# Two trunk layers in one kernel: grouped RWKV state products, values in the activation ring, reordered first loads, last gain on ScalarE

## The chip, the cores and the metric

The kernel runs on one core of one Trainium2 chip. The metric is the device time of one execution in microseconds; lower is better. The engines are TensorE (PE in the profile, PEld its weight loads), VectorE (DVE), ScalarE (ACT), GpSimd (POOL) and SyncE (SP, which only issues transfers here).

## What is computed

A sequence of 512 tokens of width 1024 goes through two layers, in float32. Each layer adds to the residual stream h a token mixer, a cross attention to a memory of 256 tokens, and a gated feed-forward block (1024 to 2 x 2752 and back, with a causal convolution of three taps). The first mixer is a gated linear attention (GLA, 4 heads) beside RWKV-7 (8 heads of 64); the second is an RG-LRU beside an mLSTM. The parts that the change touches are, cut to what matters:

```python
mem_n = rms_norm(mem, mem_norm_g)
# rwkv7_chunked, chunks of 64 tokens, per head:
rhs = concat([a_dec, A_ak @ v])
sol = triangular_solve(I - A_ab, rhs)
def step(S, inp):
    z = z_state @ S + z_local
    y = r_dec @ S + A_rb @ z + y_local
    S = S * decay + z^T b_end + v^T k_end
# the end of the trunk:
return rms_norm(h, final_norm_g)
```

## The kernel before

Activations lie transposed: a tile holds 128 features (partitions) by 512 tokens. A dense product is made of blocks: `block` (L261) loads one weight block of 128 x 1024 with `wload` (L240), which splits it into a rounded high part (`wh`, on ACT) and a remainder (`wl`, on DVE), and `dense` (L252) adds 24 products of 128 x 512 into a PSUM bank, three for each of eight feature tiles. A block's raw weights lie in a ring of 3 buffers (`wr`, "raw"), the parts in a ring of 2 (`wh`, `wl`), the PSUM banks of dense products in a ring of 3 (`mm`); 5 more banks (`ax`) serve everything else. Activations of the mixers lie in a ring of 16 buffers (`qr`, named "xs").

The program is written as straight Python, and a list scheduler puts the instructions of each engine into an order when the kernel is built: an instruction whose inputs and buffers are there by the scheduler's own reckoning goes next, earlier program text first. `issue_after(ins)` adds an edge: what is traced under it stands behind `ins` on the same engine. On the chip each engine and each transfer queue runs its order without looking ahead.

The stages that the change touches, in the order of time:

- Start (`Trunk.__init__` L144 to L183, `trunk` L1239 to L1269). SP loads the vector table, the first tile of x, the first weight block `wk` of 512 KB, then x1 to x7. POOL issues the load of `cmat` (identity, `bo64`, `rmask`). Ten products of `ones_d` by itself (L170) keep PE at work before the first weights are there. DVE scales `bo64` into `bo64m` (L178). Then `gla` (L593) runs, for each of eight feature tiles of x, two small "stacked" products and three of the first block; next come the sums of squares of x (`squares`, L1259), the reciprocal norm `rstd`, and `al` (tile "alr", L627), which frees a PSUM bank.
- The RWKV preparation (L800 to L869), four times, once for a pair of heads: blocks for r, k and v, gates, decays by a scan on DVE, score products. v is written into a zero-padded tile `vp` (L798, one buffer) at an offset of 64 columns, and nine transposes of overlapping windows (L832 to L839) bring the values of both heads into the tiles `SV`, by five copies on ACT. `during(p)` (L1281) puts other work in between: `memory_norm` (L484) loads four tiles of the memory, squares them on ACT and adds the squares on DVE, with its scratch in the `qr` ring.
- A triangular solve on DVE (L880 to L909) beside the key and value products of the memory.
- The state recurrence (L917 to L949): eight chunks, one after the other. A chunk has four groups of eight small products, over `p` (four pairs of heads) and `e` (the two heads of a pair): w (L922), the first part of y (L927), z (L931), uu (L938) and the last part of y (L947, which adds to the same bank as L927). z goes back into `SV[0]` by a DVE copy and into `SV[1]` by an ACT copy (L932, L933). A float32 product is two instructions in the trace, so a group is 16. Beside the recurrence PE works on dense products of the memory (`memory_k`, `memory_v`, called from `after`, L1293), which the scheduler puts between the groups.
- The end (`ffn` with `out`, L386 to L396, and `finish`, L1336). The last output block is made in two halves of 256 tokens. For each, `finish` forms the norm and multiplies eight tiles by gain and norm (L1347, eight DVE instructions of 128 x 256), and every second one issues a store of two tiles, in turn from SP and ACT.

Of the kernel before, what the change touches and what calls it, by code (L numbers as in the profile page):

```python
# [8 lines left out]
F32 = mybir.dt.float32  # L9
F32R = mybir.dt.float32r  # L10
U8 = mybir.dt.uint8
AF = mybir.ActivationFunctionType
ALU = mybir.AluOpType
# [4 lines left out]
P = 128  # L18
T = 512
# [123 lines left out]
class Trunk:  # L143
    def __init__(self, ctx, tc, I):  # L144
        self.tc, self.nc, self.I = tc, tc.nc, I
        nc = tc.nc
        self.con = self.pool(ctx, "con", 1)
        self.wr = self.pool(ctx, "wr", 3)
        self.wh = self.pool(ctx, "wh", 2)
        self.pr = (self.pool(ctx, "pa", 8), self.pool(ctx, "pb", 8))  # L150
        self.qr = self.pool(ctx, "qr", 16)
        self.mm = self.pool(ctx, "mm", 3, space=PSUM)
        self.ax = self.pool(ctx, "ax", 5, space=PSUM)
        self.dram = self.pool(ctx, "dr", 1, space=DRAM)
        con = self.con
        self.vec = con.tile([P, NVEC], F32, name="vec")
        nc.sync.dma_start(out=self.vec, in_=I["vec"])
        self.cm = con.tile([P, 384], F32, name="cmat")
        nc.gpsimd.dma_start(out=self.cm, in_=I["cmat"][:, 0:384])
        self.ident = self.cm[:, 0:128]  # L160
        self.bo64 = self.cm[:, 128:256]
        self.rmask = self.cm[:, 256:384]
        self.ones = {}
        for n, v in (("d", 1.0 / D), ("h", 1.0 / P)):
            t = con.tile([P, P], F32, name="ones_" + n)
            nc.gpsimd.memset(t, v)
            self.ones[n] = t

        warm = self.mm.tile([P, T], F32, name="mm")
        for i in range(10):  # L170
            self.mmul(warm[:, 0:P], self.ones["d"], self.ones["d"])
        self.cols = {}
        for n, v in (("eps", EPS), ("one", 1.0), ("gn", 64 * 1e-5), ("l2", 1e-12), ("tiny", 2e-38)):
            t = con.tile([P, 1], F32, name="col_" + n)
            nc.gpsimd.memset(t, v)
            self.cols[n] = t
        self.bo64m = con.tile([P, P], F32, name="bo64m")
        nc.vector.tensor_scalar(out=self.bo64m, in0=self.bo64, scalar1=1.0 / 64.0, scalar2=None, op0=ALU.mult)  # L178
        self.u = []
        for i in range(2):  # L180
            t = con.tile([P, T + 4], F32, name=f"upad{i}")
            nc.gpsimd.memset(t[:, 0:4], 0.0)
            self.u.append(t)  # L183
# [53 lines left out]
                self.nc.scalar.preload_act_table_set(name)  # L237


    def wload(self, src, kb, m):  # L240
        nc = self.nc
        raw = self.wr.tile([P, 1024], F32, name="raw")
        hi = self.wh.tile([P, 1024], F32R, name="wh")
        lo = self.wh.tile([P, 1024], F32R, name="wl")
        n = kb * m
        self.last_load = nc.sync.dma_start(out=raw[:, :n], in_=src.rearrange("p k m -> p (k m)"))
        self.act(hi[:, :n], raw[:, :n], AF.Copy)
        self.tt(lo[:, :n], raw[:, :n], hi[:, :n].bitcast(F32), ALU.subtract)
        sh = lambda t: t[:, :n].rearrange("p (k m) -> p k m", m=m)
        return sh(hi), sh(lo)  # L250

    def dense(self, ps, W, X, first=True, last=True):  # L252
# [43 lines left out]
class Norm:  # L296
# [5 lines left out]
    def feed(self, k, h):  # L302
        if self.ring is not None:
            self.operand(k, h)
        self.square(h)
# [178 lines left out]
def memory_norm(K, sm):  # L484

    nc = K.nc
    src = K.I["memT"].rearrange("(k p) m -> p k m", p=P)
    pair = lambda t: t.rearrange("p (k m) -> p k m", m=256)
    acc, M = sm.tile([P, T], F32, name="nacc"), []
    for i in range(4):  # L490
        f = K.qr.tile([P, T], F32, name="xs")
        nc.sync.dma_start(out=pair(f), in_=src[:, 2 * i:2 * i + 2])
        M.append(f)
        sq = K.qr.tile([P, T], F32, name="xs") if i else acc
        K.act(sq, f, AF.Square)
        if i:
            K.add(acc, acc, sq)
    yield M
    ps = K.mm.tile([P, T], F32, name="mm")
    for i in range(2):  # L500
        K.mmul(ps[:, 0:256], K.ones["d"], acc[:, i * 256:(i + 1) * 256], i == 0, i == 1)
    r = K.qr.tile([P, T], F32, name="xs")[:, 0:256]
    K.act(r, ps[:, 0:256], AF.Ln, bias=K.cols["eps"])
    K.act(r, r, AF.Exp, scale=-0.5)
    for k in range(KD):
        f = pair(M[k // 2])[:, k % 2]
        K.stt(f, f, K.v("mem_norm_g", k), r, ALU.mult, ALU.mult)
    yield M
# [84 lines left out]
def gla(K, nm, wga, wk, squares, after, Y):  # L593
    nc, X = K.nc, nm.X
    with ExitStack() as es:
# [4 lines left out]
        nc.gpsimd.dma_start(out=gf, in_=K.I["cmat"][:, 1024:1152].rearrange("p (o m) -> p o m", o=1))  # L600
        with K.tc.issue_after(after.ins):
            nc.vector.tensor_copy(out=gm, in_=gf)
        wa = gp.tile([48, 256], F32, name="walpha")
        nc.gpsimd.memset(wa, 0.0)
        for r in (0, 32):
# [147 lines left out]
def shifted(K, out, ps, i, om):  # L753

    K.act(out, ps, AF.Copy, scale=om[:, i:i + 1])
    K.stt(out[:, 1:], ps[:, 0:T - 1], K.v("rwkv_mu", i), out[:, 1:], ALU.mult, ALU.add)
    return out
# [9 lines left out]
def rwkv(K, X, Y, during, after):  # L767
# [3 lines left out]
    with ExitStack() as core:  # L771
# [12 lines left out]
        with ExitStack() as es:  # L784
# [10 lines left out]
            gl = shifted(K, new(), K.block("w_rw", 13, X), 13, om)  # L795
            sigmoid(K, glr, gl, scale=-1.0)
            reset = reset_mask(K, wt, 65)
            vp = wt.tile([P, 640], F32, name="vp")  # L798
            nc.gpsimd.memset(vp, 0.0)
            for p in range(4):  # L800
                r = shifted(K, new(), K.block("w_rw", p, X), p, om)
                k = shifted(K, new(), K.block("w_rw", 4 + p, X), 4 + p, om)
                v = shifted(K, vp[:, 64:576], K.block("w_rw", 8 + p, X), 8 + p, om)
                ps = K.ax.tile([P, T], F32, name="ax")
                psa = K.ax.tile([P, T], F32, name="ax")
                K.mmul(ps, w2a2[0:64, p * P:(p + 1) * P], wa[0:64])
# [22 lines left out]
                for e in range(2):  # L829
                    K.stt(stk[e][R[e], p, :, 0:64], c8(kn)[R[e]], -1.0, e1[R[e], :, 0:64], ALU.mult, ALU.mult)  # L830
                    K.mul(stk[e][R[e], p, :, 64:128], c8(r)[R[e]], e1[R[e], :, 1:])
                for w0, w1 in ((0, 4), (4, 8), (8, 9)):  # L832
                    ps = K.ax.tile([P, 4, P], F32, name="ax")
                    for w in range(w0, w1):
                        nc.tensor.transpose(ps[:, w - w0], vp[:, w * 64:w * 64 + P], K.ident)
                    if w0 < 8:
                        K.act(SV[0][64:128, w0:w1, p], ps[64:128, :, 0:64], AF.Copy)
                    w = max(w0, 1)
                    K.act(SV[1][0:64, w - 1:w1 - 1, p], ps[0:64, w - w0:w1 - w0, 64:128], AF.Copy)  # L839
                K.mul(kn, kn, a)  # L840
                K.act(a, a, AF.Identity, scale=K.v("rwkv_k_a", p), bias=om[:, 14 + p:15 + p])
                K.mul(k, k, a)
# [67 lines left out]
        with ExitStack() as es:  # L910
# [3 lines left out]
            for e in range(2):  # L914
                nc.vector.memset(SV[e][R[e], 0], 0.0)
            yt = [st.tile([P, T], F32, name=f"y{p}", bufs=1) for p in range(4)]
            for c in range(8):  # L917
                w = K.ax.tile([P, 4, 64], F32, name="ax")
                yp = K.ax.tile([P, 4, 64], F32, name="ax")
                for p in range(4):  # L920
                    for e in range(2):
                        K.mmul(w[R[e], p], stk[e][:, p, c, 0:64], SV[e][:, c, p])  # L922
                ws = st.tile([P, 4, 64], F32, name="ws")
                nc.vector.tensor_copy(out=ws, in_=w)
                for p in range(4):
# [7 lines left out]
                K.act(SV[1][R[1], c], z[R[1]], AF.Copy)  # L933
                if c < 7:
                    uu = K.ax.tile([P, 4, 64], F32, name="ax")
                    for p in range(4):
                        for e in range(2):
                            K.mmul(uu[R[e], p], BKT[:, p, c, R[e]], SV[e][:, c, p])  # L938
                    t = st.tile([P, 4, 64], F32, name="t")
                    K.add(t, S, uu)  # L940
                    sb = sdt[:, c].rearrange("p (a o) -> p a o", o=1)
                    for e in range(2):
                        K.mul(SV[e][R[e], c + 1], t[R[e]], sb[R[e]].to_broadcast([64, 4, 64]))
                    K.mul(S, t, sb.to_broadcast([P, 4, 64]), nc.gpsimd)
                for p in range(4):
                    for e in range(2):
                        K.mmul(yp[R[e], p], SV[e][R[e], c, p], BB[R[e], p, c, 64:128], False, p == 3)  # L947
                for p in range(4):
                    K.act(yt[p][:, c * 64:c * 64 + 64], yp[:, p], AF.Copy)  # L949
            g2 = K.qr.tile([P, T], F32, name="xs")  # L950
# [288 lines left out]
def trunk(tc, I, out):  # L1239
    nc = tc.nc  # L1240
    with ExitStack() as ctx:
        K = Trunk(ctx, tc, I)
        sm = K.pool(ctx, "nsm", 1)
        with ExitStack() as es:
# [4 lines left out]
            load = lambda k: nc.sync.dma_start(out=x[k], in_=I["xT"][k * P:(k + 1) * P])  # L1249
            load(0)  # L1250
            alpha = stacked_weights(K, I["w_ga"][:, 0], 16, 32, nt.tile([P, KD * 48], F32R, name="walr", bufs=1), nc.scalar)
            wk = K.wload(I["w_gla"][:, 2], KD, P)
            for k in range(1, KD):
                load(k)
            K.exp_ln()
            for k in range(KD):
                last = nm.operand(k, x[k])
# [50 lines left out]
        for l in range(2):  # L1308
# [23 lines left out]
            else:  # L1332
# [3 lines left out]
                def finish(s, ps):  # L1336
# [6 lines left out]
                    K.mmul(ms, K.ones["d"], r, False, True)  # L1343
                    K.act(r, ms, AF.Ln, bias=K.cols["eps"])
                    K.act(r, r, AF.Exp, scale=-0.5)
                    for j in range(KD):
                        K.stt(h[j][:, s], h[j][:, s], K.v("final_norm_g", j), r, ALU.mult, ALU.mult)  # L1347
                        if j % 2:
                            (nc.sync, nc.scalar)[j // 2 % 2].dma_start(out=dst[:, j - 1:j + 1, s],
                                                                      in_=ht[:, j - 1:j + 1, s])  # L1350

                ffn(K, l, nf, h, nm.feed, finish)


# [13 lines left out]
```

## Time and profile before

| | us |
|---|---|
| median of 3 runs | 1558.81 (1558.35 to 1563.36) |
| the profiled execution's own time | 1558.83 |
| its span, first to last instruction | 1557.0 |
| PE busy in the span | 1527.6 |
| DVE busy | 914.9 |
| ACT busy | 683.7 |
| mean granted TensorE clock | 0.996 |

A busy PE in this profile is one on which a product is in flight; between products that follow each other at once there is no idle time, whatever each costs. So the cost of a product within a stream is read from the start of one to the start of the next, and a change of its cost doesn't show as idle time. The granted clock is 1.00 at 2.4 GHz and 0.50 at 1.2 GHz; a value between is a stretch with some of each.

### The profile page before, as it was taken

How to read it: one execution, taken by the hardware profiler on the slowest of the kernel's cores; microseconds unless marked ns; L12 is line 12 of the kernel's file. 1: busy time of each engine (PE TensorE's matmuls, PEld its weight loads, DVE VectorE, ACT ScalarE, POOL GpSimd, SP SyncE). 2: the span in 40 equal slices, each digit the busy share in tenths (PEclk: the TensorE clock that was granted, in tenths of full speed). 3: DMA queues.
4: the chain of work that ended last, by engine and by line, in shares of the span. 5: the costliest groups of instructions: out<-in, count | busy, mean ns of one | idle time of the engine just before them, and what ended most of it. 6: DMA issues, size and time to landing. Idle time of an engine off the chain costs nothing.

```text
span 1557.0 us, 20187 instructions
## 1 busy us (share of the span) xinstructions
PE 1527.6 (98%) x8077; PEld 1240.3 (80%) x8077; DVE 914.9 (59%) x1348; ACT 683.7 (44%) x1101; POOL 23.3 (1%) x62
## 2 busy tenths in 40 slices
PE   8999999999999999999999999999999999999997
PEld 6876777787888888888888878788888888888886
DVE  7537679645655755556633386777557556565333
ACT  5465563345444543333332267566345333333221
POOL 2000000001000000000000000000000000000000
PEclk9999999999999999999999999999999999999999
DMA  4222226226331333332233321224213333322332
GB/s 165 81 75 82 68 62 192 90 93 224 111 106 48 107 97 98 99 95 95 92 98 102 94 98 49 75 73 149 72 51 117 105 98 95 96 95 89 101 98 78
DMA packets 50175, 152.19 MB, mean 98 GB/s; under 512 B 5505, under 2 KB 8865, under 8 KB 50081
## 3 DMA queue, kind: packets, MB, share of 16 engines
q1 hardware_dynamic: 45664, 142.87, 29.2%
q10 hardware_dynamic: 3536, 5.38, 1.0%
q0 software_dynamic: 880, 2.66, 0.4%
q8 instruction: 63, 1.03, 0.3%
q14 instruction: 32, 0.25, 0.1%
HBM read 144.59 MB, written 6.29 MB: 97 GB/s over the span
## 4 chain that ended last, share of the span: by engine, by line
PE 89%; DVE 6%; ACT 3%; DMA 1%; issue 1%; SPq 0%; DVEq 0%; ACTq 0%
PE mm L209 77%; PE ax L209 10%; DVE wl L194 1%; ACT e L206 1%; PE ax L453 1%; ACT wh L206 1%; DVE tm L194 1%; DVE bb L892 0%; DVE tu L194 0%; DMA raw<-in_w_kv 0%; DMA raw<-in_w_gla 0%; DVE au L881 0%; DVE e L814 0%; ACT a L206 0%; DVE stk L203 0%
## 5 line engine op out<-in xcount | busy, mean ns | idle before, releaser
L209 PE MATMUL mm<-xs,wh 128*128 128x512 f32 (+1 forms) x3627 | 1110.4, 387 | 2.4 <-DVE vp L203 1.8
L209 PEld LDWEIGHTS mm<-xs,wh 128*128 128x128 f32 x3627 | 671.8, 188 | 147.9 <-issue 8.0
L209 PE MATMUL mm<-xs,wl 128*128 128x512 f32 (+1 forms) x1814 | 700.3, 386 | 0.6 <-DVE wl L194 0.5
L206 ACT ACTIVATE wh<-raw 128x1024 fp32r<-128x1024 f32 (+2 forms) x273 | 264.8, 970 | 528.5 <-PE mm L209 412.1
L194 DVE TENSOR_TENSOR wl<-raw,wh 128x1024 fp32r<-128x1024 f32 (+2 forms) x272 | 302.6, 1113 | 211.8 <-ACT wh L206 210.8
L209 PEld LDWEIGHTS mm<-xs,wl 128*128 128x128 f32 x1814 | 341.0, 188 | 71.9 <-issue 1.8
L194 DVE TENSOR_TENSOR upad<-mm,rstd 128x512 f32<-128x512 f32 (+1 forms) x52 | 35.9, 690 | 95.5 <-PE mm L209 95.3
L194 DVE TENSOR_TENSOR h<-h,mm 128x512 f32<-128x512 f32 (+1 forms) x73 | 49.5, 677 | 69.3 <-PE mm L209 69.1
L194 DVE TENSOR_TENSOR g<-mm,rstd 128x512 f32<-128x512 f32 (+1 forms) x44 | 30.4, 692 | 76.0 <-PE mm L209 75.9
L203 DVE SCALAR_TENSOR_TENSOR c<-upad,vec,c 128x512 f32<-128x512 f32 (+1 forms) x88 | 65.9, 749 | 3.3 <-ACT c L206 1.8
L209 PE MATMUL mm<-wh,xs 128*128 128x256 f32 (+1 forms) x256 | 66.4, 349 | 0.0
L206 ACT ACTIVATE c<-c 128x512 f32<-128x512 f32 (+1 forms) x44 | 27.8, 632 | 87.1 <-DVE c L203 87.1
L209 PEld LDWEIGHTS mm<-wh,xs 128*128 128x128 f32 x256 | 44.8, 194 | 6.3 <-issue 1.0
L209 PE MATMUL mm<-wl,xs 128*128 128x256 f32 (+1 forms) x128 | 45.3, 354 | 3.8 <-DVE wl L194 3.8
L206 ACT ACTIVATE xs<-g 128x512 fp32r<-128x512 f32 (+1 forms) x44 | 27.8, 633 | 26.9 <-DVE g L194 26.9
L206 ACT ACTIVATE c<-upad,vec 128x512 f32<-128x512 f32 (+1 forms) x44 | 35.3, 802 | 1.5 <-DVE upad L194 1.5
L206 ACT ACTIVATE e<-ax,mx,scl 128x256 f32<-128x256 f32 x32 | 17.8, 560 | 39.8 <-DVE mx L194 39.8
L194 DVE TENSOR_TENSOR g<-c,g 128x512 f32<-128x512 f32 (+1 forms) x44 | 30.4, 692 | 5.8 <-ACT c L206 1.4
L194 DVE TENSOR_TENSOR nacc<-nacc,nsq 128x512 f32<-128x512 f32 x45 | 32.8, 730 | 0.3
L203 DVE SCALAR_TENSOR_TENSOR xs<-h,vec,xs 128x512 fp32r<-128x512 f32 x40 | 29.9, 749 | 3.5 <-ACT xs L206 3.4
L194 DVE TENSOR_TENSOR xs<-ax,xs 128x512 fp32r<-128x512 f32 x32 | 21.3, 687 | 18.0 <-ACT xs L206 18.0
L206 ACT ACTIVATE xs<-h,vec 128x512 fp32r<-128x512 f32 x40 | 28.8, 719 | 6.5 <-DVE h L194 6.5
(353 smaller groups left out, 1221.9 us busy)
## 6 DMA issues: line engine op xcount, KB each, us to landing
raw<-in_w_up SPq DMA_DIRECT2D x86, 512.0 KB, 3.4
raw<-in_w_dn SPq DMA_DIRECT2D x32, 512.0 KB, 3.4
raw<-in_w_kk SPq DMA_DIRECT2D x16, 512.0 KB, 3.6
raw<-in_w_kv SPq DMA_DIRECT2D x16, 512.0 KB, 3.9
raw<-in_w_q SPq DMA_DIRECT2D x16, 512.0 KB, 3.6
raw<-in_w_o SPq DMA_DIRECT2D x32, 256.0 KB, 2.6
raw<-in_w_cd SPq DMA_DIRECT2D x16, 512.0 KB, 3.2
raw<-in_w_rw SPq DMA_DIRECT2D x14, 512.0 KB, 3.6
```

The costliest lines, as they stand in the source:

```text
L194: (eng or self.nc.vector).tensor_tensor(out=out, in0=a, in1=b, op=op)
L203: return self.nc.vector.scalar_tensor_tensor(out=out, in0=a, scalar=s, in1=b, op0=op0, op1=op1)
L206: return self.nc.scalar.activation(out=out, in_=a, func=f, **kw)
L209: self.last_mm = self.nc.tensor.matmul(out, lhsT=l, rhs=r, start=start, stop=stop)
L453: nc.tensor.transpose(pT[m][:, t * P:(t + 1) * P], e[:, i, m * P:(m + 1) * P], K.ident)
```

## The change

1. Start: `cmat` is loaded by SP behind x7 instead of by POOL at the beginning; the first weight block comes in two halves of 256 KB, with x1 issued between them and x2 behind them; each half has its own split on ACT and DVE; 16 warming products instead of 10; `bo64m` is made behind the GLA mask.
2. RWKV values: v lies in the `qr` ring, four transposes of disjoint windows replace nine, four copies on ACT replace five.
3. `memory_norm` takes its scratch (three squares and the norm) from the raw weight ring.
4. State products: the groups w, uu and last y put the head e=1 first, and the other seven products of a group get an edge behind the first.
5. End: the final gain is applied to tiles 0 to 6 by ACT when they are fed (after their squares), and `finish` multiplies by the norm alone in three instructions of 3, 3 and 1 tiles, plus one for tile 7; stores are of 3, 3 and 2 tiles.

```diff
@@ Trunk.__init__
-        nc.gpsimd.dma_start(out=self.cm, in_=I["cmat"][:, 0:384])
-        for i in range(10):
+        for i in range(16):
-        nc.vector.tensor_scalar(out=self.bo64m, in0=self.bo64, scalar1=1.0 / 64.0, scalar2=None, op0=ALU.mult)
@@ wload
+    def wload(self, src, kb, m, parts=1, between=None):
...
+        n = kb * m // parts
+        src = src.rearrange("p k m -> p (k m)")
+        for i in range(parts):
+            s = slice(i * n, (i + 1) * n)
+            self.last_load = nc.sync.dma_start(out=raw[:, s], in_=src[:, s])
+            if between:
+                between(i)
+        for i in range(parts):
+            s = slice(i * n, (i + 1) * n)
+            self.act(hi[:, s], raw[:, s], AF.Copy)
+            self.tt(lo[:, s], raw[:, s], hi[:, s].bitcast(F32), ALU.subtract)
@@ memory_norm
-        sq = K.qr.tile([P, T], F32, name="xs") if i else acc
+        sq = K.wr.tile([P, 1024], F32, name="raw")[:, :T] if i else acc
-    r = K.qr.tile([P, T], F32, name="xs")[:, 0:256]
+    r = K.wr.tile([P, 1024], F32, name="raw")[:, 0:256]
@@ gla, behind the mask's tensor_copy, in the same issue_after
+            nc.vector.tensor_scalar(out=K.bo64m, in0=K.bo64, scalar1=1.0 / 64.0, scalar2=None, op0=ALU.mult)
@@ rwkv, preparation
-            vp = wt.tile([P, 640], F32, name="vp")
-            nc.gpsimd.memset(vp, 0.0)
-                v = shifted(K, vp[:, 64:576], K.block("w_rw", 8 + p, X), 8 + p, om)
+                v = shifted(K, new(), K.block("w_rw", 8 + p, X), 8 + p, om)
-                for w0, w1 in ((0, 4), (4, 8), (8, 9)):
-                    ps = K.ax.tile([P, 4, P], F32, name="ax")
-                    for w in range(w0, w1):
-                        nc.tensor.transpose(ps[:, w - w0], vp[:, w * 64:w * 64 + P], K.ident)
-                    if w0 < 8:
-                        K.act(SV[0][64:128, w0:w1, p], ps[64:128, :, 0:64], AF.Copy)
-                    w = max(w0, 1)
-                    K.act(SV[1][0:64, w - 1:w1 - 1, p], ps[0:64, w - w0:w1 - w0, 64:128], AF.Copy)
+                ps = K.ax.tile([P, 4, P], F32, name="ax")
+                for t in range(4):
+                    nc.tensor.transpose(ps[:, t], v[:, t * P:(t + 1) * P], K.ident)
+                for e in range(2):
+                    for i in range(2):
+                        K.act(SV[e][R[1 - e], i::2, p], ps[R[i], :, R[e]], AF.Copy)
@@ rwkv, recurrence
+            def group(products):
+                products[0]()
+                with K.tc.issue_after(K.last_mm.ins):
+                    for f in products[1:]:
+                        f()
-                for p in range(4):
-                    for e in range(2):
-                        K.mmul(w[R[e], p], stk[e][:, p, c, 0:64], SV[e][:, c, p])
+                group([lambda e=e, p=p: K.mmul(w[R[e], p], stk[e][:, p, c, 0:64], SV[e][:, c, p])
+                       for p in range(4) for e in (1, 0)])
...
@@ trunk
-            wk = K.wload(I["w_gla"][:, 2], KD, P)
-            for k in range(1, KD):
+            rest = iter(range(1, KD))
+            wk = K.wload(I["w_gla"][:, 2], KD, P, 2, lambda i: load(next(rest)))
+            for k in rest:
                 load(k)
+            nc.sync.dma_start(out=K.cm, in_=I["cmat"][:, 0:384])
@@ finish, and the feed of the last ffn
-                    for j in range(KD):
-                        K.stt(h[j][:, s], h[j][:, s], K.v("final_norm_g", j), r, ALU.mult, ALU.mult)
-                        if j % 2:
...
+                    rb = r.rearrange("p (o m) -> p o m", o=1)
+                    for a, b in ((0, 3), (3, 6), (6, 8)):
+                        c = min(b, KD - 1)
+                        K.mul(ht[:, a:c, s], ht[:, a:c, s], rb.to_broadcast([P, c - a, 256]))
+                        if b > c:
+                            K.stt(h[c][:, s], h[c][:, s], K.v("final_norm_g", c), r, ALU.mult, ALU.mult)
+                        (nc.scalar if a == 3 else nc.sync).dma_start(out=dst[:, a:b, s], in_=ht[:, a:b, s])
+                def feed(j, t):
+                    nm.feed(j, t)
+                    K.act(t, t, AF.Copy, scale=K.v("final_norm_g", j))
```

## Rows read from the trace of the kernel before

**Rows 1.** The page's part 1: busy us, share of the span, instructions.

```profile
PE 1527.6 (98%) x8077; PEld 1240.3 (80%) x8077; DVE 914.9 (59%) x1348; ACT 683.7 (44%) x1101; POOL 23.3 (1%) x62
```

**Rows 2.** Timeline of the start: us, length, engine, line, operation, [idle before <-releaser].

```profile
2.23 4.64 PE L209 MATMUL mm<-ones_d 128*128 128x128 f32 x20 [2.23 <-POOL ones_d L166]
...
7.72 0.23 DVE L178 TENSOR_SCALAR bo64m<-cmat 128x128 f32<-128x128 f32 x1 [7.72 <-DMA cmat<-in_cmat]
...
8.73 1.06 ACT L206 ACTIVATE wh<-raw 128x1024 fp32r<-128x1024 f32 x1 [3.56 <-DMA raw<-in_w_gla]
...
11.10 0.80 PE L209 MATMUL mm<-xs,wl 128*128 128x512 f32 x1 [0.52 <-DVE wl L194]
...
26.03 0.68 DVE L194 TENSOR_TENSOR alr<-mm,rstd 48x512 f32<-48x512 f32 x1 [1.68 <-ACT rstd L206]
```

**Rows 3.** Busy time in windows of 2 us at the start, with granted clock.

```profile
10.00:12.00 2.00, 1.48 (x4) 0.74 (x5) 2.00 (x3) 2.00 (x4) 0.00 (x0) 0.68 1.06 413
12.00:14.00 2.00, 2.00 (x6) 1.17 (x5) 2.00 (x4) 2.00 (x4) 0.00 (x0) 0.50 1.03 421
```

**Rows 4.** Transfers issued in the first 30 us: KB each, median us to landing.

```profile
x<-in_xT SPq DMA_DIRECT2D x8, 256.0 KB, 7.6
```

**Rows 5.** The page's part 6, weight loads of two sizes over the whole kernel.

```profile
raw<-in_w_q SPq DMA_DIRECT2D x16, 512.0 KB, 3.6
raw<-in_w_o SPq DMA_DIRECT2D x32, 256.0 KB, 2.6
```

**Rows 6.** PE's timeline in the RWKV preparation: nine transposes and what follows.

```profile
145.37 1.15 PE L835 MATMUL ax<-cmat,vp 128*128 128x128 f32 x9
146.27 0.47 PE L209 MATMUL mm<-xs,wl 128*128 128x512 f32 x1
```

**Rows 7.** PE's timeline in GLA: four transposes and what follows.

```profile
38.23 0.64 PE L662 MATMUL ax<-cmat,ke 128*128 128x128 f32 x4
38.62 0.47 PE L209 MATMUL mm<-xs,wh 128*128 128x512 f32 x1
```

**Rows 8.** PE's longest wait on v's tile, 84 to 232 us: total, times, longest.

```profile
PE mm L209 <- DVE vp L203: 1.8, 1, 1.8
```

**Rows 9.** Timeline beside the memory norm: a weight load and its split.

```profile
139.75 0.34 SPq L246 DMA_DIRECT2D raw<-in_w_rw  x1
...
149.08 1.05 ACT L206 ACTIVATE wh<-raw 128x1024 fp32r<-128x1024 f32 x1
150.17 1.23 DVE L194 TENSOR_TENSOR wl<-raw,wh 128x1024 fp32r<-128x1024 f32 x1
```

**Rows 10.** PE's timeline in the state recurrence, one chunk.

```profile
292.26 0.33 PE L209 MATMUL ax<-sv,bkt 128*64 128x64 f32 x2
292.52 0.33 PE L209 MATMUL ax<-bb,sv 64*64 64x64 f32 x2
292.78 0.51 PE L209 MATMUL mm<-wh,xs 128*128 128x512 f32 x1
...
293.92 0.68 PE L209 MATMUL ax<-sv,bkt 128*64 128x64 f32 x14
...
295.13 0.50 PE L209 MATMUL mm<-wl,xs 128*128 128x512 f32 x1
...
296.26 0.40 PE L209 MATMUL ax<-sv,stk 128*64 128x64 f32 x3
...
297.47 0.49 PE L209 MATMUL mm<-wh,xs 128*128 128x512 f32 x1
```

**Rows 11.** Busy time in the recurrence and behind it (columns as in rows 3).

```profile
290.00:338.00 48.00, 48.00 (x648) 39.66 (x645) 22.61 (x38) 15.49 (x43) 5.09 (x6) 1.00 0.29 89
```

**Rows 12.** The end: DVE's last work, a remainder of 128 x 768, and a window.

```profile
1537.79 0.96 DVE L194 TENSOR_TENSOR wl<-raw,wh 128x768 fp32r<-128x768 f32 x1 [3.87 <-ACT wh L206]
...
1550.36 3.25 DVE L203 SCALAR_TENSOR_TENSOR h<-h,vec,nsq 128x256 f32<-128x256 f32 x8 [2.19 <-ACT nsq L206]
...
1553.00:1554.00 1.00, 0.00 (x0) 0.00 (x0) 0.61 (x2) 0.00 (x0) 0.00 (x0) 0.77 0.95 338
```

More of the change, by code (lines that the diff above doesn't have):

```diff
@@ L237, in exp_ln @@
                 self.nc.scalar.preload_act_table_set(name)
-    def wload(self, src, kb, m):
+    def wload(self, src, kb, m, parts=1, between=None):
         nc = self.nc
@@ L244, in wload @@
         lo = self.wh.tile([P, 1024], F32R, name="wl")
[L245 to L249, printed above, removed]
+        n = kb * m // parts
[9 more added lines that the diff above has]
+            self.tt(lo[:, s], raw[:, s], hi[:, s].bitcast(F32), ALU.subtract)
+        sh = lambda t: t[:, :kb * m].rearrange("p (k m) -> p k m", m=m)
         return sh(hi), sh(lo)
@@ L935, in rwkv @@
                     uu = K.ax.tile([P, 4, 64], F32, name="ax")
-                    for p in range(4):
-                        for e in range(2):
-                            K.mmul(uu[R[e], p], BKT[:, p, c, R[e]], SV[e][:, c, p])
+                    group([lambda e=e, p=p: K.mmul(uu[R[e], p], BKT[:, p, c, R[e]], SV[e][:, c, p])
+                           for p in range(4) for e in (1, 0)])
                     t = st.tile([P, 4, 64], F32, name="t")
@@ L944, in rwkv @@
                     K.mul(S, t, sb.to_broadcast([P, 4, 64]), nc.gpsimd)
-                for p in range(4):
-                    for e in range(2):
-                        K.mmul(yp[R[e], p], SV[e][R[e], c, p], BB[R[e], p, c, 64:128], False, p == 3)
+                group([lambda e=e, p=p: K.mmul(yp[R[e], p], SV[e][R[e], c, p], BB[R[e], p, c, 64:128], False, p == 3)
+                       for p in range(4) for e in (1, 0)])
                 for p in range(4):
@@ L1345, in finish @@
                     K.act(r, r, AF.Exp, scale=-0.5)
-                    for j in range(KD):
-                        K.stt(h[j][:, s], h[j][:, s], K.v("final_norm_g", j), r, ALU.mult, ALU.mult)
-                        if j % 2:
-                            (nc.sync, nc.scalar)[j // 2 % 2].dma_start(out=dst[:, j - 1:j + 1, s],
-                                                                      in_=ht[:, j - 1:j + 1, s])
-                ffn(K, l, nf, h, nm.feed, finish)
+                    rb = r.rearrange("p (o m) -> p o m", o=1)
[8 more added lines that the diff above has]
+                    K.act(t, t, AF.Copy, scale=K.v("final_norm_g", j))
+                ffn(K, l, nf, h, feed, finish)
 def kernel(**inputs):
```

## The prediction, made before the changed kernel ran

> **What bounds the kernel now.** I read the busy times of the engines first: PE has work in flight for 1527.6 us [rows 1] of a span of 1557.0, so 29.4 us of idle time is all that a better order alone could win, unless products become cheaper or the clock higher. DVE and ACT have room on the whole, but not in every stage. So I looked at each stage that the change touches with the timeline, and asked two things: what do PE's products cost there from start to start, and whose work does PE wait for. At the start the reader is to see the first weights landing late [rows 2] and the clock at its lower level [rows 3]; in the RWKV preparation the price of transposes [rows 6, 7]; in the recurrence groups of products that are cut in two [rows 10] while PE is never idle [rows 11]; at the end DVE's eight multiplications ahead of the last stores [rows 12].
>
> **Start.** Before: the products begin in earnest at 11.10, behind the split of the first block, whose load landed at 8.7 and kept ACT idle for 3.56 us; the warming products had ended at 6.9 [rows 2]. The granted clock then was 0.68 from 10 to 12 us and 0.50 from 12 to 14 [rows 3]: that is the lower level (1.2 GHz) for (1 - 0.68) / 0.5 x 2 + 2 = 3.3 us, after an interval in which PE had little to do; about half of it, 1.6 us, is lost work. Six more warming products at 4.64 / 10 = 0.46 us each last until at most 9.7, or 8.2 if the later ones run at the upper level. If real products follow directly, PE is some 2 us early and loses no clock: 2 to 4 us at that point. But this is not what ends last. The reciprocal norm ends the stretch: "alr" at 26.03 waited for it [rows 2], its PSUM bank is needed for the next block, and it hangs on the sums of squares, which hang on ACT's eight conversions of x, which on ACT stand behind the first block's split at 8.73. With a half landing earlier, ACT moves up by between 0 (the half lands no earlier, or x7 decides) and 3.56 us (all its wait). I take the middle, **-1.8 us**.
>
> The transfers that are moved: x1 goes ahead of the second half and x2 to x7 stand one issue later; `cmat` leaves POOL's queue, where the mask and alpha weights move up, and goes to the end of SP's, ahead of the second weight block. A transfer in that crowd takes 7.6 us [rows 4], so a `cmat` issued at about 8.7 lands by about 16.3. `bo64m` no longer holds DVE from 0 to 7.72 [rows 2], but behind the mask it can hold up DVE's adds of the squares; they had 26.03 - 16.3 us to the norm, so I cost that at nothing, with up to 1 us if `cmat` slips.
>
> One row speaks against the halves. In a quiet stretch 512 KB take 3.6 us and 256 KB 2.6 [rows 5]: halving the size saves 1.0 us, not half. The Trainium skill, DMA: Bandwidth & Descriptors, "Anatomy of one DMA", says the same more strongly: a transfer has a fixed part of about 2 us, which a split pays twice. By its formula a half would land about 0.6 us sooner (an estimate from that page), and the start would be worth that, the sum 1.2 us less.
>
> **RWKV preparation.** Nine transposes take 146.27 - 145.37 = 0.90 us of PE from start to start [rows 6]; four take 38.62 - 38.23 = 0.39 [rows 7]. Four pairs of heads: 4 x 0.51 = 2.0 us less of PE's work. v's single buffer also goes: PE waited 1.8 us once because the block of v could not leave its bank [rows 8]; bounds 0 and 1.8, I take half, 0.9, since other instructions stand ahead of v on ACT too. ACT's five copies become four; it is not what ends there. A ring slot more for v (three released by the scratch) could bring a new wait in the fourth pair; the old buffer imposed the same wait, so nothing. Sum **-2.9 us**.
>
> **Scratch in the weight ring.** It costs nothing as long as weights arrive early. Cover: the load issued at 139.75 was split from 149.08 on [rows 9], 9.3 us, of which landing takes 3.6 [rows 5]; 5.7 us are slack, and a square and an add hold a buffer for under 2. What is queued behind it on SP is the next weight load, and PE waits for that one. Without the cover each load costs 3.6 + 1.05 + 1.23 = 5.9 us.
>
> **Recurrence.** In a chunk the first product of uu and of the last y (two instructions each, e=0, ready when DVE has copied z) go out alone at 292.26 and 292.52, then dense work from 292.78 until ACT has copied the other half, and the remaining 28 from 293.92 to 295.13 [rows 10]. The isolated ones cost 0.52 us, the 28 cost 1.21. A group that is not cut shows what they would cost together: w and the first y, all 32 instructions, take 297.47 - 296.26 = 1.21 [rows 10]. The two isolated products would be free: 7 chunks with uu x 0.52 = 3.6 us. Their order makes e=1 first, the later one to be ready, so the other seven follow without a wait. w is cut in some later chunks too; between 0 and 7 x 0.26 = 1.8 us, half is 0.9. PE has no idle time here [rows 11], and what isn't done beside the recurrence is done behind it, so I count it all: **-4.5 us**, bounds 0 and -5.4.
>
> **End.** DVE's eight instructions take 3.25 us; three tiles at once about 0.96 by the 128 x 768 row, so 0.96 + 0.96 + 0.41 + 0.41 = 2.7 [rows 12], 0.5 less. But the first store now leaves 0.14 us later (three tiles against two), and the transfers are busy to 0.95 at 338 GB/s in the window behind it [rows 12], so the stores themselves decide much of the end. Bounds +0.1 and -0.5, I take **-0.2 us**. The seven ACT copies lie in a stage where PE decides and ACT is idle more than half of the time [rows 1]: nothing.
>
> **Sum.** -1.8 - 2.9 - 4.5 - 0.2 = -9.4 us. The profiled execution took 1558.83, practically the median of the three runs (1558.81), so no correction: **1549.4 us**.
>
> **Rivals.** (a) The recurrence gives nothing: the edges only put seven products behind the first, and the scheduler may still set dense work between them, or the dense work that it sets beside the chain is too short by its own reckoning and PE idles in the time won. For it: the cuts come from that scheduler's order. Against: with e=1 first, nothing remains to wait for. Then -9.4 + 4.5 = -4.9: 1553.9.
> (b) The halves land no sooner, or x7 decides: the start gives 0 instead of -1.8, and the waits on v's buffer stay (0.9): 1552.1. The page named above is on this side. Against: ACT's 3.56 us of idle time.
> (c) Slower: the scratch takes the raw buffers at the wrong moment. Three squares and a norm each hold one of three buffers behind a load of the memory, SP's order puts a weight load behind each, and PE starves for the whole way of a load, 5.9 us, three times: 17.7, with the clock's fall after such a stall 1.6 more [rows 3]: 1549.4 + 19.3 = 1568.7. It decides from two and a half starved loads on (14.1 us, which is 9.4 + 4.7). Against it stands the slack of 5.7 us.
>
> **Chances and range.** About 0.3%, 4.7 us, is what a measurement of this kernel can tell from no change; faster means below 1554.1. Forecast 0.60, (a) 0.17, (b) 0.15, (c) 0.08. Around the forecast the bounds give -5.4 - 3.8 - 3.6 - 0.5 = -13.3 as the most, 1545.5; a shift of the scheduler's whole order adds a little on both sides. (a) lies on the border: 0.09 faster, 0.08 same; (b) 0.12 faster, 0.03 same; the forecast 0.57 faster, 0.03 same. So 0.78 faster, 0.14 same, 0.08 slower. The range reaches over (a) and (b): 1544.5 to 1556.5.
>
> **What would show it.** Right: first products of the first block before 10 us and a granted clock of 1.00 from 10 to 14; "alr" near 24; four transposes a pair and no wait on v; in the recurrence groups of 16 with 1.21 us for 32 instructions and no group of 2 instructions; behind it everything early by the sum. Wrong: PE idle in front of weights between 110 and 232 us; a lower clock anywhere new; new idle time in the recurrence; or an unchanged distance between "alr" and the first product.

## The result, and the profile after

The changed kernel takes 1576.23 us (median of 4 runs, 1575.16 to 1584.87), the kernel before, run beside it, 1558.58 (4 runs, 1557.69 to 1563.36): ratio 1.0119, 95% interval 1.0078 to 1.016. The forecast was 1549.4 with a range of 1544.5 to 1556.5: the change was to save 9.4 us and costs some 18. Its profiled execution is the longest of the four (1584.87, span 1583.1).

The page's part 1 of the changed kernel, to be set beside [rows 1]:

```profile
PE 1537.1 (97%) x8069; PEld 1249.1 (79%) x8069; DVE 914.6 (58%) x1341; ACT 690.6 (44%) x1105; POOL 22.6 (1%) x60
```

PE's idle time was 29.4 us; now it is 1583.1 - 1537.1 = 46.0. To see where it arose, I took one event that all kernels have, DVE's first transpose of the triangular solve behind the RWKV preparation (`au<-bb`), and "alr", the end of the start stretch. Timeline of DVE, before and then after:

```profile
233.04 1.98 DVE L881 STREAM_TRANSPOSE au<-bb 128x1024 f32<-128x1024 f32 x1
```
```profile
24.00 0.68 DVE L192 TENSOR_TENSOR alr<-mm,rstd 48x512 f32<-48x512 f32 x1 [1.47 <-ACT rstd L204]
...
258.24 1.95 DVE L884 STREAM_TRANSPOSE au<-bb 128x1024 f32<-128x1024 f32 x1
```

The solve begins 25.2 us later than before, though the start was 2.0 us earlier (26.03 in [rows 2]); from the solve to the end the two spans are nearly the same, 1557.0 - 233.0 = 1324.0 and 1583.1 - 258.2 = 1324.9. So the loss shows between 24 and 258 us, in GLA and the RWKV preparation, where the change takes 27.2 us longer. Some 7.6 of these are a stretch at the lower clock from about 68 to 85 us, ahead of every wait named below, which most of the other profiles don't have (last section); 19.6 are left to explain. The gain of the recurrence lies behind the solve and doesn't show in these two spans, so something is lost there too; the last experiment says what. The windows of the preparation, changed kernel (PE, PEld, DVE, ACT, POOL busy with counts, granted clock, DMA share, GB/s):

```profile
84.00:130.00 46.00, 37.32 (x196) 28.93 (x198) 19.10 (x28) 25.89 (x40) 0.81 (x4) 0.91 0.10 29
130.00:160.00 30.00, 20.76 (x117) 15.24 (x111) 13.89 (x18) 14.45 (x25) 0.00 (x0) 0.78 0.34 105
160.00:226.00 66.00, 60.39 (x362) 45.24 (x362) 44.43 (x63) 39.93 (x70) 0.22 (x2) 0.99 0.17 50
...
120.00:140.00 20.00, 8.45 (x78) 5.69 (x78) 14.13 (x20) 11.63 (x24) 0.11 (x1) 0.74 0.00 1
140.00:160.00 20.00, 14.71 (x54) 11.60 (x55) 7.93 (x11) 8.63 (x13) 0.00 (x0) 0.75 0.51 157
...
220.00:225.70 5.70, 1.02 (x4) 0.30 (x2) 5.03 (x11) 5.70 (x11) 0.00 (x0) 0.94 0.05 6
225.70:232.00 6.30, 6.28 (x15) 4.93 (x16) 2.23 (x2) 1.93 (x5) 0.00 (x0) 0.51 0.72 244
```

There are two holes: one from about 119 to 145, up to 140 of which the transfers move nothing (share 0.00), and one from 220 to 225.7; behind the second the clock is at its lower level (0.51). PE's waits with their releasers, and SP's queue, tell what was missing. Timeline of PE, then waits of SP's queue, then timeline of SP's issues, all of the changed kernel:

```profile
127.44 1.51 PE L207 MATMUL ax<-stk,bk 64*64 64x128 f32 x10 [8.52 <-issue]
...
145.26 1.22 PE L207 MATMUL mm<-xs,wh 128*128 128x512 f32 x2 [9.20 <-ACT wh L204]
...
224.31 0.72 PE L207 MATMUL mm<-xs,wh 128*128 128x512 f32 x2 [4.02 <-ACT wh L204]
```
```profile
SPq L248 <- DVE nacc L192: 45.7, 3, 44.4
...
SPq L248 <- DVE xs L201: 23.7, 1, 23.7
```
```profile
39.85 25.36 SPq L248 DMA_DIRECT2D raw<-in_w_rw  x5
93.75 0.33 SPq L799 DMA_DIRECT2D w2a<-in_w_w2a  x1
94.13 1.96 SPq L498 DMA_DIRECT2D xs<-in_memT  x4
140.62 2.46 SPq L248 DMA_DIRECT2D raw<-in_w_rw  x3
146.49 2.93 SPq L248 DMA_DIRECT2D raw<-in_w_gla  x2
```

("issue" means that the profile shows no releaser. The product at 127.44 is a score product; DVE made its `bk` from 126.64 to 127.33, and without a weight block PE had nothing to do meanwhile.)

From 65 to 140 us no load into the weight ring goes out. The next one waits 44.4 us for DVE's `nacc`, the add that reads a square of the memory norm and so frees its raw buffer. When that add comes is decided by ACT's order, in which the squares stand behind the second pair's gate work. Timeline of ACT and DVE there:

```profile
137.49 0.67 ACT L204 ACTIVATE a<-ax,neg 128x512 f32<-128x512 f32 x1
...
138.58 0.62 ACT L204 ACTIVATE nacc<-xs 128x512 f32<-128x512 f32 x1
139.10 0.62 ACT L204 ACTIVATE raw<-xs 128x512 f32<-128x512 f32 x1
...
139.93 0.67 DVE L192 TENSOR_TENSOR nacc<-nacc,raw 128x512 f32<-128x512 f32 x1
```

The memory tiles were asked for at 94.13, and the transfers were idle from 100 on; the squares were done 40 us later only because ACT had been given other work first. In the kernel before, five weight loads went out between 91.82 and 113.9, ahead of the first memory tiles at 124.33. Timeline of SP's issues before:

```profile
91.82 11.21 SPq L246 DMA_DIRECT2D raw<-in_w_rw  x3
108.14 5.76 SPq L246 DMA_DIRECT2D raw<-in_w_gla  x2
...
124.33 1.45 SPq L492 DMA_DIRECT2D xs<-in_memT  x3
```

The three squares take all three raw buffers one behind the other, so they are a barrier in the ring: no weight load behind them can be issued before the squares are done. The norm `r` does it once more, 23.7 us for SP and 4.02 for PE.

### The profile page after: what moved, and what is told of

The parts are those of the page before. It is cut to its first block, busy times and chain, and to the rows that moved or that the text cites. A ratio compares the mean times of both kernels' runs of the same rounds, so it can differ in the third digit from the quotient of the medians.

```text
span 1583.1 us, 20157 instructions
## 1 busy us (share of the span) xinstructions
PE 1537.1 (97%) x8069; PEld 1249.1 (79%) x8069; DVE 914.6 (58%) x1341; ACT 690.6 (44%) x1105; POOL 22.6 (1%) x60
## 4 chain that ended last, share of the span: by engine, by line
PE 88%; DVE 6%; ACT 3%; DMA 1%; issue 1%; SPq 0%; POOL 0%; DVEq 0%; ACTq 0%
PE mm L207 77%; PE ax L207 11%; DVE wl L192 1%; ACT wh L204 1%; PE ax L459 1%; DMA raw<-in_w_kv 1%; DVE tu L192 0%; DVE tm L192 0%; ACT xs L204 0%; DVE au L884 0%; DMA x<-in_xT 0%; ACT e L204 0%; PE ax L862 0%; DMA lgw<-in_w_lg 0%; DVE stk L201 0%
## 5 line engine op out<-in xcount | busy, mean ns | idle before, releaser
L192 DVE TENSOR_TENSOR h<-h,mm 128x512 f32<-128x512 f32 (+1 forms) x73 | 49.4, 677 | 70.0 <-PE mm L207 69.8
L192 DVE TENSOR_TENSOR xs<-ax,xs 128x512 fp32r<-128x512 f32 (+1 forms) x36 | 24.0, 685 | 18.0 <-ACT xs L204 18.0
L192 DVE TENSOR_TENSOR xs<-g,xs 128x512 fp32r<-128x512 f32 (+1 forms) x44 | 30.1, 685 | 2.5 <-ACT xs L204 2.5
```

The costliest lines, as they stand in the source:

```text
L192: (eng or self.nc.vector).tensor_tensor(out=out, in0=a, in1=b, op=op)
```

## The experiments

Theory A, formed from these rows: the scratch in the weight ring costs all that was lost, some 20 us, and the rest of the change gains. Rival B: the other parts lose too, or the loss is one of the clock. Here and below "the change" is the changed kernel.

**The scratch put back, in the change.**

```diff
-        sq = K.wr.tile([P, 1024], F32, name="raw")[:, :T] if i else acc
+        sq = K.qr.tile([P, T], F32, name="xs") if i else acc
...
-    r = K.wr.tile([P, 1024], F32, name="raw")[:, 0:256]
+    r = K.qr.tile([P, T], F32, name="xs")[:, 0:256]
```

> The changed kernel with the memory norm's scratch (three squares and the norm) back in the qr ring; all else as changed. Theory A, scratch in the weight ring: the three squares held all three raw buffers until 139.9 us and the norm held one until 224 us, so SP issued no weight load from 96 to 140 us; without them PE has no wait of over 2 us between 110 and 232 us, and the time falls from 1576.2 to between 1547 and 1556 us. Theory B, another order: the other parts gave the scheduler another order (v in the ring, first loads), and the waits come from that; then the time stays above 1565 us, with PE's waits still there.

Measured: 1556.92 us (12 runs), ratio to before 0.9979 (0.9961 to 0.9998). That is just above the 1556 at which theory A's range ended, and one wait of PE of 5.6 us is left, where theory A had none over 2. Two lines of the scratch are worth 1576.2 - 1556.9 = 19.3 us by the medians, and by the two ratios (1.0119 and 0.9979) 1.4%, some 22 us. Its windows, beside those of the change above:

```profile
84.00:130.00 46.00, 45.06 (x251) 35.15 (x250) 26.39 (x38) 28.23 (x45) 0.81 (x4) 1.00 0.30 86
130.00:160.00 30.00, 24.42 (x147) 17.30 (x146) 20.09 (x28) 18.39 (x34) 0.11 (x1) 0.89 0.24 71
160.00:226.00 66.00, 64.97 (x365) 49.11 (x367) 44.08 (x63) 39.95 (x70) 0.11 (x1) 1.00 0.22 64
```

PE is busy 134.45 us of these 142, against 118.47 in the change: 16.0 us are idle time. The rest of the 19.3 is probably the lower clock behind the holes (0.75 from 140 to 160 and 0.51 from 225.7 to 232, above); no run separates it. But with 0.2% this kernel gains far less than the other terms promised, so they too had to be measured.

**The scratch alone, in the kernel before**: the same two lines the other way round.

> The kernel before with the scratch alone moved into the weight ring. Theory A: the same starving, 18 to 28 us more than before, 1576 to 1587 us, with a hole in the weight loads of 30 us or more ahead of the second pair of heads. Theory B: 1556 to 1562 us.

Measured: 1584.54 (4 runs), ratio 1.0148 (1.0125 to 1.017). The move alone costs 23 us and needs none of the other parts. SP's queue shows the same wait:

```profile
SPq L246 <- DVE nacc L194: 45.0, 3, 43.7
```

**The squares back, the norm left in the ring; and the other way round.**

```diff
-        sq = K.wr.tile([P, 1024], F32, name="raw")[:, :T] if i else acc
+        sq = K.qr.tile([P, T], F32, name="xs") if i else acc
```

> The changed kernel with only the three squares back in the qr ring; the norm of the memory stays in a raw buffer. Theory A: the hole ahead of the second pair goes (two waits of PE of 8.5 and 9.2 us and the lower clock behind them, 16 to 20 us in all), the smaller one near 225 us stays (4 to 6 us): 1553 to 1560 us. Theory B: above 1565 us.

```diff
-    r = K.wr.tile([P, 1024], F32, name="raw")[:, 0:256]
+    r = K.qr.tile([P, T], F32, name="xs")[:, 0:256]
```

> The changed kernel with only the norm of the memory back in the qr ring; the three squares stay in raw buffers. Theory A: the hole ahead of the second pair stays, the wait near 225 us goes: 1569 to 1573 us. Theory B: no change from 1576 us.

Measured: with the norm alone in the ring 1560.9 (10 runs), ratio 1.0012 (0.9989 to 1.0035); with the squares alone 1575.79 (4 runs), ratio 1.0087 (1.0057 to 1.0116). PE's waits from 84 us to the solve, first of the one, then of the other:

```profile
PE mm L207 <- DVE xs L201: 5.6, 1, 5.6
PE mm L207 <- ACT wh L204: 4.0, 1, 4.0
```
```profile
PE mm L207 <- ACT wh L204: 9.5, 1, 9.5
PE ax L207 <- issue: 8.5, 1, 8.5
```

By the waits, the squares make the first hole and the norm the second, each alone as in the change. By the medians they cost about 19 us (1575.8 - 1556.9) and 4 (1560.9 - 1556.9). Both times miss theory A's ranges: 1560.9 is a little above the 1560 of the one, and 1575.8 is what theory B had expected of the other, no change from 1576. It is the traces that decide here, since the wait near 225 us is gone with the norm put back. The profile of that version has the stretch at the lower clock named above (69.70 us from "alr" to SP's load of `w2a`, last section); its one run at a mean clock of 0.986 took 1571.06.

**The start alone, in the kernel before.**

```diff
-        for i in range(10):
+        for i in range(16):
...
-            wk = K.wload(I["w_gla"][:, 2], KD, P)
-            for k in range(1, KD):
+            rest = iter(range(1, KD))
+            wk = K.wload(I["w_gla"][:, 2], KD, P, 2, lambda i: load(next(rest)))
+            for k in rest:
...
+            nc.sync.dma_start(out=K.cm, in_=I["cmat"][:, 0:384])
...
```

> The kernel before with the new start alone (order of loads, halves, 16 warming products, bo64m). As predicted: alr 1.8 us or more ahead of before and the same off the time, -1.5 to -3 us. Rival: the profiled execution of before had a late start (the kernel with the scratch alone moved, whose start is the old one, had alr at 24.14 us against 26.03), so the start itself is worth at most 0.7 us: -1.0 to +0.5 us.

Measured: 1557.96 (12 runs), ratio 0.9999 (0.9981 to 1.0017): nothing that can be measured. The interval is from -3.0 to +2.6 us, so these times alone would not exclude the 1.8 us that were foretold.

**The new values alone, in the kernel before.**

```diff
...
-                v = shifted(K, vp[:, 64:576], K.block("w_rw", 8 + p, X), 8 + p, om)
+                v = shifted(K, new(), K.block("w_rw", 8 + p, X), 8 + p, om)
...
+                ps = K.ax.tile([P, 4, P], F32, name="ax")
+                for t in range(4):
+                    nc.tensor.transpose(ps[:, t], v[:, t * P:(t + 1) * P], K.ident)
...
```

> The kernel before with the RWKV values alone changed (v in the qr ring, four transposes); the scratch stays in qr. As predicted: 2.0 us of PE's work and up to 1.8 us of waits less, -2 to -4 us. Rival, the ring: v takes a slot of the qr ring that a tile of the memory needs, its load comes late and PE waits about 6 us ahead of the second pair, as in the changed kernel with its scratch put back: -1 to +4 us, with a wait of PE on xs in the trace.

Measured: 1561.97 (12 runs), ratio 1.0025 (1.0006 to 1.0045), slower if anything. PE's longest wait in the preparation, with before's in [rows 8]:

```profile
PE mm L209 <- DVE xs L203: 5.5, 1, 5.5
```

The transposes are saved and the 1.8 us wait on v's old buffer is gone, but a wait of 5.5 us has taken its place; it is also in the change with its scratch put back (5.6).

**The groups alone, in the kernel before.**

```diff
+            def group(products):
+                products[0]()
+                with K.tc.issue_after(K.last_mm.ins):
+                    for f in products[1:]:
+                        f()
...
-                for p in range(4):
-                    for e in range(2):
-                        K.mmul(w[R[e], p], stk[e][:, p, c, 0:64], SV[e][:, c, p])
+                group([lambda e=e, p=p: K.mmul(w[R[e], p], stk[e][:, p, c, 0:64], SV[e][:, c, p])
+                       for p in range(4) for e in (1, 0)])
...
```

> The kernel before with the grouped state products alone. As predicted: 32 products of a pair of groups in 1.2 us, chunks of 6.8 us instead of 7.6, and 3.6 to 5.4 us off the time. Rival, clock: the stretch from the solve to the first chunks is at the lower clock for 10 us or more instead of 7 and takes half of it back: -2 to +1 us.

Measured: 1552.54 (12 runs), ratio 0.9955 (0.9938 to 0.9972), some 7 us, with an interval of 4.4 to 9.7 that reaches into the 3.6 to 5.4 expected. The edges and the order of `e` were not tried apart. PE's timeline of one chunk, to be set beside [rows 10]:

```profile
292.91 0.69 PE L209 MATMUL ax<-sv,bkt 128*64 128x64 f32 x16
293.53 0.68 PE L209 MATMUL ax<-bb,sv 64*64 64x64 f32 x16
294.14 0.50 PE L209 MATMUL mm<-wh,xs 128*128 128x512 f32 x1
...
295.49 0.69 PE L209 MATMUL ax<-sv,stk 128*64 128x64 f32 x16 [0.15 <-DVE sv L194]
```

All 32 products go out together in 294.14 - 292.91 = 1.23 us, and no group of two is left. The copies of w to `ws`, one a chunk, give the length of the whole recurrence (the tile's view: durations, first and last start), before and then with the groups:

```profile
L924 DVE COPY ws<-ax x8: 363/425/426, 282.4 to 335.1; 128x256 f32<-128x256 f32 x8
```
```profile
L931 DVE COPY ws<-ax x8: 364/426/426, 281.6 to 329.2; 128x256 f32<-128x256 f32 x8
```

Seven chunks take 47.6 us instead of 52.7: 5.1 us less. In the change itself they take 48.2 (309.2 to 357.4).

**A buffer of its own for the scratch, in the change**: 2 KB a partition, in the pool of the RWKV stage's weights.

```diff
...
-        sq = K.wr.tile([P, 1024], F32, name="raw")[:, :T] if i else acc
+        sq = own.tile([P, T], F32, name="msq") if i else acc
...
-    r = K.wr.tile([P, 1024], F32, name="raw")[:, 0:256]
+    r = own.tile([P, T], F32, name="msq")[:, 0:256]
...
```

> The changed kernel with the memory norm's scratch in one buffer of its own (2 KB a partition, in the place that the padded tile of v left), in neither ring. Theory ring: without the scratch in the qr ring the last tiles of the memory are loaded in time, the wait of about 6 us ahead of the second pair (seen with the scratch back in qr) goes or halves, and the time is 2 to 5 us below that version, 1551 to 1555 us. Rival: v alone fills the ring, the wait stays, and the time is the same as with the scratch in qr, 1555 to 1559 us.

Measured: 1552.97 (9 runs, 1544.64 to 1554.64), ratio 0.9953 (0.9935 to 0.9971): faster than both kernels. PE's longest wait from 84 us to the solve is the shortest of all (1.7 us in total, two times, the longest 1.1):

```profile
PE ax L207 <- DVE bk L192: 1.7, 2, 1.1
```

So neither the weight ring nor the ring of values has to carry the scratch.

**Groups, end and start, in the kernel before; neither the new values nor the scratch.** The hunks are those of the diff.

> Left out of the change: the new tile for v (v keeps its padded buffer and its nine transposes a pair) and the move of memory_norm's scratch; start, groups and end are new. Theory (the new values gain nothing as long as v takes a slot of the ring, since memory tiles 3 and 4 then load late; groups and end are the whole gain, and the start is worth nothing): groups alone measured 1552.5, the end 0.2 less, so 1552.3, within 1550 to 1554, below the change with its scratch put back (1556.9) by some 4 us. No product from 84 us to the solve waits more than 2 us for a shifted value. Rival (the transposes saved are worth 2 us after all and only the clock differs between those runs): 1556 to 1560.

Measured: 1552.66 (12 runs), ratio 0.9956 (0.9937 to 0.9975), the same as the groups alone: the start and the end add nothing that can be measured. PE's longest wait is again the one on v's buffer, 1.8 us.

**v in one unpadded buffer of its own, the scratch back in the ring of values, in the change.**

```diff
...
-                v = shifted(K, new(), K.block("w_rw", 8 + p, X), 8 + p, om)
+                v = shifted(K, wt.tile([P, T], F32, name="vv", bufs=1), K.block("w_rw", 8 + p, X), 8 + p, om)
```

> The change with memory_norm's scratch back in the ring of values and v in one buffer of its own of 2 KB, unpadded: four transposes a pair stay, the ring slot that v took is free again. Theory (what the new values lose is the ring slot: memory tiles 3 and 4 wait for it, the block of r waits for them behind ACT's squares, 5.5 us of PE): the memory loads go out at about 125 to 129, the 5.5 us wait for a shifted value at 141 is gone, and a wait on v's single buffer of up to 1.8 us comes back; 1551 to 1555, like the change with its scratch in a buffer of its own (1553.0). Rival (the ring slot is not it; the evictions are late for another cause, such as the copies of the new transposes): still 5 us of waits for shifted values, 1556 to 1559.

Measured: 1551.87 (9 runs), ratio 0.9941 (0.9921 to 0.9962), the lowest of all, though the intervals of the last four experiments overlap. The long wait is half as long:

```profile
136.92 0.70 PE L207 MATMUL mm<-xs,wh 128*128 128x512 f32 x2 [2.71 <-DVE vv L201]
```

but not by the mechanism that was expected. The last memory loads go out at 130.25 here and at 130.20 in the change with its scratch put back, and no earlier; the ring slot does not move them. What differs is v's eviction on ACT. In the change with its scratch put back, first, r's, k's and v's stand together behind a square that waits for its memory tile; here, second, v's is done ahead of that square:

```profile
134.65 0.63 ACT L204 ACTIVATE xs<-xs 128x512 f32<-128x512 f32 x1 [0.68 <-DMA xs<-in_memT]
...
138.20 1.83 ACT L204 ACTIVATE xs<-mm,om 128x512 f32<-128x512 f32 x3
```
```profile
134.05 0.69 ACT L204 ACTIVATE vv<-mm,om 128x512 f32<-128x512 f32 x1
134.76 0.63 ACT L204 ACTIVATE xs<-xs 128x512 f32<-128x512 f32 x1
```

That this order is the cause is read from two traces and was not tried by itself.

From "alr" to the solve it takes 226.92 - 23.48 = 203.4 us, the kernel of the experiment before this one, with the old values, 231.29 - 23.98 = 207.3: the preparation is 3.9 us shorter. The whole kernel isn't. From "alr" to the end it is 1547.2 - 23.5 = 1523.7 against 1549.7 - 24.0 = 1525.7, 2.0 us less. The rest is work put off: PE's records, of which some can be missing, hold 997 products on the banks `mm` from "alr" to the last copy to `ws` here and 1021 there, which is a block of 24 less, and from that copy to the end it takes 1225.5 us here and 1221.5 there. All seven kernels with the new values are like this (1224.8 to 1226.0). The four with the old values and the scratch in the ring of values take 1221.5 to 1221.9, the one with the scratch alone moved 1228.1. In the change this is most of what hides the recurrence's gain.

## Why the prediction was wrong, step by step

**Scratch in the weight ring: the step that failed.** It said that the scratch "costs nothing as long as weights arrive early", since "a square and an add hold a buffer for under 2" us against 5.7 of slack. The work takes under 2 us, but the buffer is not held for the length of the work. Its turn in the ring comes when the block that had the buffer last has been split, and it is free again when the add has run, which hangs on when ACT's order comes to the square: at 139, some 40 us after the memory tiles had landed. The slack was read beside one load of the kernel before [rows 9], in which nothing of the kind stood in the ring; three squares in a ring of three leave no load ahead at all. It was also read wrongly: counted from the start, the load at 139.75 is SP's 21st into the ring and the split at 149.08 is the 19th, of the load at 123.96, and both loads were split 25.1 us after their issue (the later one at 164.82). So the cover before was larger than the 9.3 us of the prediction; in the change it was gone. The right question was what stands ahead of the squares on ACT. Rival (c) had the place and the kind, "SP's order puts a weight load behind each", and its price, 17.7 + 1.6 = 19.3 us, is what the scratch cost by the medians. That the two agree so closely is luck: the waits were 8.5, 9.2 and 4.0 us instead of three of 5.9, and they came from one barrier of 44.4 us on SP's queue and one of 23.7, not from single loads that started late. It came to 1568.7 where 1576.2 was measured mainly because the rest of the change, with the scratch put back, saves 0.21% (0.02 to 0.39), some 3 us, instead of 9.4. Its chance of 0.08 was far too small: the 5.7 us of slack were taken as evidence against it.

**RWKV preparation, -2.9 foretold.** Four transposes a pair are there, and the 1.8 us wait on v's buffer went. But the sentence that a ring slot more for v "could bring a new wait in the fourth pair; the old buffer imposed the same wait, so nothing" failed: the new wait is 5.5 us, it comes ahead of the second pair, and the part alone measured +0.25% (+0.06 to +0.45). With a buffer of its own for v the term is 2.0 us from "alr" to the end in the profiles, the 2.0 of the transposes without the 0.9 for the wait (one of 2.71 is left); the runs, 0.9941 against 0.9956, can't tell it from nothing.

**Recurrence, -4.5 foretold.** The mechanism was right: 5.1 us in the chunk distances and 7 (4.4 to 9.7) in the runs of the part alone, so 4.5 is within what was measured. Rival (a) was wrong: what remains ahead of a group is 0.15 to 0.26 us.

**Start, -1.8 foretold.** The signs came as described: in the change the first products of the first block start at 7.80, and the clock is at 1.00 where [rows 3] have 0.68 and 0.50. But they don't show what the new start does, because [rows 2] are of a late execution. The kernel with the scratch alone moved has the old start, and it converts the first block, in one piece, almost when the change converts the first half, and at the same clock. Conversion and window, that kernel first, then the change:

```profile
6.26 1.06 ACT L206 ACTIVATE wh<-raw 128x1024 fp32r<-128x1024 f32 x1 [0.98 <-DMA raw<-in_w_gla]
...
10.00:12.00 2.00, 2.00 (x10) 1.34 (x9) 1.94 (x3) 2.00 (x5) 0.00 (x0) 1.00 1.05 422
```
```profile
6.10 0.63 ACT L204 ACTIVATE wh<-raw 128x512 fp32r<-128x512 f32 x1 [0.96 <-DMA raw<-in_w_gla]
...
10.00:12.00 2.00, 2.00 (x10) 1.18 (x9) 2.00 (x4) 2.00 (x5) 0.00 (x0) 1.00 1.06 410
```

So most of the 1.8 was not there to be won. The three kernels with the scratch, the values or the groups alone, all with the old start, begin this conversion at 6.26, 6.33 and 6.86 and have "alr" at 24.14, 24.20 and 24.40, against 8.73 and 26.03 in [rows 2]. The eight profiles with the new start begin it from 5.22 to 6.16 and have "alr" from 23.43 to 24.37, 23.88 in the mean. The halves come 0.8 us sooner in the mean, and the start gains 0.4 us. Rival (b) was right about the start's price, but not about the halves, which do land sooner. The formula in the Trainium skill, DMA: Bandwidth & Descriptors, "Anatomy of one DMA", had given 0.6; the traces agree with it roughly, though that section is about transfers issued by GpSimd and these are SP's. The step that failed here is the reading of one execution's first microseconds as what the old start costs.

**End, -0.2 foretold.** In the change DVE's last work is 2.16 + 0.48 = 2.6 us against 3.25 [rows 12]; the three instructions that multiply by the norm alone:

```profile
1576.67 2.16 DVE L192 TENSOR_TENSOR h<-h,nsq 128x768 f32<-128x768 f32 x3 [2.19 <-ACT nsq L204]
```

From PE's product over the last sum of squares (`ax<-nacc,ones_d`, at 1573.86; before at 1547.54) to the end of the span it is 9.24 us, before 9.46: 0.2, as foretold, in one profile of each.

**The sum without the step that failed.** With the scratch in its own buffer the change gains 0.47% (0.29 to 0.65), 7 us (4.5 to 10), where 9.4 were foretold: 9.4 lies within the interval. The start's 1.4 us too many would be over half of the difference.

## What to carry to other kernels

A buffer borrowed from a prefetch ring is held from its turn in the ring to the end of the borrower, not for as long as the borrower works; if the borrower waits behind other work on an in-order engine, every load behind it on the queue waits too, and as many borrowers as the ring has buffers stop the prefetch altogether. Before scratch is moved into such a ring, look at what stands ahead of the borrower on its engine, and give it 2 KB of its own where they are to be had. And before a term is taken from one profiled stretch at the start of a kernel, it is well to know how much that stretch varies between executions.

## What the runs showed of the hardware

The clock can differ between executions of one order of instructions. From 62 to 72 us the change with its scratch put back and the one with its own scratch buffer have the same products in the same order on PE, with the same two short waits (0.57 and 0.17 us) just ahead; their windows, the first kernel and then the second:

```profile
66.00:72.00 6.00, 6.00 (x62) 4.09 (x57) 4.48 (x14) 0.28 (x1) 0.00 (x0) 1.00 0.20 76
72.00:80.00 8.00, 8.00 (x82) 6.47 (x80) 1.41 (x3) 3.61 (x6) 0.00 (x0) 1.00 0.01 2
```
```profile
66.00:72.00 6.00, 6.00 (x48) 3.69 (x49) 4.07 (x12) 0.28 (x1) 0.00 (x0) 0.65 0.22 76
72.00:80.00 8.00, 8.00 (x49) 7.07 (x49) 0.77 (x3) 0.43 (x1) 0.00 (x0) 0.50 0.01 2
```

The change's own profile has such a spell too; by SP's load of `w2a`, 69.75 us behind "alr" there against 62.16 with the scratch put back, it cost 7.6 us. That execution is 8.6 us above the median at a mean clock of 0.980, the other three have 0.984; whether they lack the spell is not recorded. By the same distance, three of the twelve profiles have it in full (69.7 to 69.8 us), one in part (65.7), and eight have none (62.2 to 62.8). Runs of one kernel spread by as much with their mean clock: the one with its own scratch buffer took 1544.64 at 0.996 and 1554.64 at 0.99. What sets off a spell is open.
